# A hybrid mLSTM and gated-delta block on one core: weights loaded by half chunks, with four raw tiles and four pairs of split tiles

## The chip, the core and the metric

The kernel runs on one core of a Trainium2 chip, with its five engines: TensorE (PE in the profile, its weight loads PEld) for matrix products, VectorE (DVE), ScalarE (ACT), GpSimd (POOL) and SyncE (SP), which in this kernel issues nearly all loads of weights. Sixteen DMA engines move data between HBM and the on-chip memory SBUF. The metric is the device time of one execution in microseconds; lower is better.

## The reference, cut to what matters

One layer with 256 tokens and a width of 2048, in 32-bit floats:

```
mod = silu(c) @ W_ada + b_ada          # 6 x 2048 numbers: shift, scale, gate of both halves
h   = RMSNorm(x) * (1 + scale_m) + shift_m
proj = h @ w_in                        # q, k, v, output gate | conv input, z | gates | merge gates
y_a = bidirectional mLSTM(...)  @ w_branch_a     # 4 heads
y_b = bidirectional gated delta rule(...) @ w_branch_b   # 16 heads, chunks of 64 tokens
x  = x + gate_m * ((g_a * y_a + g_b * y_b) @ w_out)
hf = RMSNorm(x) * (1 + scale_f) + shift_f
x  = x + gate_f * ((silu(hf @ w_gate) * (hf @ w_up)) @ w_down)     # inner width 5632
```

A final RMSNorm follows. Every weight is read once: some 450 MB pass through SBUF in the course of the kernel. The last four of the six parts of `mod` belong to no early step, so their 64 MB of `W_ada` are read beside the other work.

## The kernel before, in words

**Products in three passes.** Each 32-bit weight is split into a high part and a low remainder. A load brings one *chunk* of 1 MB, 128 partitions of 8 KB, into a raw tile. Two *halves* of a chunk are then split one after the other: ScalarE copies a half (128x1024) to the high tile `wh`, and VectorE subtracts `wh` from the raw tile to get the low tile `wl`. The tokens are split in the same way (`hh`, `hl`). TensorE makes three products for each block: high by high, low by high, high by low.

**Two kinds of job.** `fjob` (lines 146 to 165) makes 128 columns for all tokens, with the weights as the loaded operand: 48 matmuls of 128x256 a chunk. `tjob` (from line 167) makes 512 columns with the tokens as the loaded operand, for two groups of 128 tokens: 24 matmuls of 128x512 a chunk, so 12 a half. Both are Python generators that yield after each half, and the rest of the program draws on them where TensorE needs work: the projections z, v, mb, o, ma, a and b are drawn between the steps of the gated delta rule. In names such as `wl_b12_1_8` stand the job (b, head 12, its second of three), and the block of the half (0 or 8 in an `fjob`, 0 or 2 in a `tjob`).

**Rings.** Tiles with one tag share a ring. Tag `raw` has 3 tiles of 8 KB a partition, tags `wh` and `wl` 3 tiles of 4 KB each. A tile is free again when its last reader is done: a raw tile after the second `wl` of its chunk, a `wh` and `wl` tile after the last matmul of the half. SP issues loads in a fixed order, so a load that waits for a raw tile holds all loads behind it.

**Modulation sums.** The parts of `mod` that are not needed early are 64 row products (`ada_part`, line 118): a 1 MB load into the same `raw` ring and one VectorE instruction at line 124, which multiplies 128x2048 weights by the broadcast row silu(c) and adds them up into one column of `mod`. `pump` (line 141) lets one of them follow every second or fourth chunk; at the output projection `wo` a table at line 1131 says after which halves one follows.

**Order.** What is marked with `order(...)` keeps the program's order on its engine; a planner with estimated costs sets the places of the rest, the splits among them. Number suffixes of names in an order listing rise in the order of the program's text.

**Stages.** 0 to 138 us: the first projection with the first two parts of `mod` (win0, `ra`, products at line 507). To 300: gates and the projections z0, v, mb. To 1000: the 16 heads of the gated delta rule in four groups; each group has an inverse of 64x64 matrices, which is solved on VectorE by repeated multiply and reduce (`uu`, lines 631 and 637) and finished by blocks on TensorE (lines 685 to 743). To 1225: mLSTM, and the projections yb and ya. To 1331: the output projection `wo`. To 1361: norm and transposes. To 2020: gate, up and down of the feed-forward part. Then a tail.

Of the kernel before, what the change touches and what calls it, by code (L numbers as in the profile page):

```python
# [24 lines left out]
KD = 11  # L25
GRP = 4
N0 = 4 + 3 * GRP


PK_ADAB = 0  # L30
# [22 lines left out]
def hybrid_block(ctx: ExitStack, tc: tile.TileContext, xr, nfr, crow, pk_d, cst_d, ada2, ada4, win0, winb, wint, wba, wbb, wo, wgu, wd, out, dbg=None):  # L53
    nc = tc.nc
# [22 lines left out]
    def both(x, kk):  # L77

        return x[:, kk // 2, :, kk % 2]
# [5 lines left out]
    def order(ins, yes=True):  # L85

        return tc.keep_in_program_order(ins) if yes else ins
# [23 lines left out]
    V.memset(row_c[:, D:], 1.0)  # L111
    def c_row(g):
        pc_ = acc_ps.tile([P, 512], F32, tag="acc", name=f"crow{g}")
        order(PE.matmul(pc_, ones[0:1], c1[:, g * 512 : (g + 1) * 512], start=True, stop=True))
        order(S.activation(row_c[:, g * 512 : (g + 1) * 512], pc_, AF.Silu))


    def ada_part(part, row_c):

        c0 = part * KB  # L120
        for b in range(KB):
            raw = st.tile([P, D], F32, tag="raw", bufs=3, name=f"ada{part}_{b}")
            nc.sync.dma_start(raw, ada4[part - 2, b])
            V.scalar_tensor_tensor(raw, raw, 1.0, row_c[:, :D], ALU.mult, ALU.mult, accum_out=mod[:, c0 + b : c0 + b + 1])  # L124
# [16 lines left out]
    def pump():  # L141
        count[0] += 1
        if every[0] and count[0] % every[0] == 0:
            sums()

    def fjob(name, src, done):

        ps = acc_ps.tile([P, 512], F32, tag="acc", name=f"acc_{name}")
        o = ps[:, :T]
        raw = st.tile([P, KB, P], F32, tag="raw", bufs=3, name=f"raw_{name}")  # L150
        nc.sync.dma_start(raw, src)
        for k0 in range(0, KB, 8):
            wh = st.tile([P, 8, P], F32R, tag="wh", bufs=3, name=f"wh_{name}_{k0}")
            wl = st.tile([P, 8, P], F32R, tag="wl", bufs=3, name=f"wl_{name}_{k0}")
            S.activation(wh, raw[:, k0 : k0 + 8], AF.Copy)  # L155
            V.tensor_tensor(wl, raw[:, k0 : k0 + 8], wh.bitcast(F32), ALU.subtract)  # L156
            for k in range(8):
                kk = k0 + k
                PE.matmul(o, wh[:, k], both(hh, kk).rearrange("p a b -> p b a"), start=kk == 0, stop=False)  # L159
                PE.matmul(o, wh[:, k], both(hl, kk).rearrange("p a b -> p b a"), start=False, stop=False)  # L160
                PE.matmul(o, wl[:, k], both(hh, kk).rearrange("p a b -> p b a"), start=False, stop=kk == KB - 1)  # L161
            if k0:
                pump()
                done(o.rearrange("p (b a) -> p a b", a=2))
            yield True

    def tjob(name, chunks, xh, xl, done, early=0, by_token=None, steps=1):

        raws = {}

        def halves(u, k0):
            if u not in raws:
                raws[u] = st.tile([P, 4, 512], F32, tag="raw", bufs=3, name=f"raw_{name}_{u}")
                nc.sync.dma_start(raws[u], chunks[u])
            wh = st.tile([P, 2, 512], F32R, tag="wh", bufs=3, name=f"wh_{name}_{u}_{k0}")
            wl = st.tile([P, 2, 512], F32R, tag="wl", bufs=3, name=f"wl_{name}_{u}_{k0}")
            order(S.activation(wh, raws[u][:, k0 : k0 + 2], AF.Copy), early)  # L180
            order(V.tensor_tensor(wl, raws[u][:, k0 : k0 + 2], wh.bitcast(F32), ALU.subtract), early)  # L181
# [12 lines left out]
        for n, (u, k0) in enumerate(todo):  # L194
            wh, wl = made.pop(0) if made else halves(u, k0)
            for k in range(2):
                kk = 4 * u + k0 + k
                for t in range(2):
                    order(PE.matmul(ps[t], tok(xh, kk, t), turns(wh[:, k]), start=kk == 0, stop=False), early and steps > 1)  # L199
                    PE.matmul(ps[t], tok(xl, kk, t), turns(wh[:, k]), start=False, stop=False)  # L200
                    PE.matmul(ps[t], tok(xh, kk, t), turns(wl[:, k]), start=False, stop=kk == last)  # L201
            if k0:
                pump()
                if u == len(chunks) - 1:
                    done(ps)
# [232 lines left out]
    with ExitStack() as s0:  # L438
# [17 lines left out]

        def loads(b):
            ra = [w0.tile([P, D + 2], F32, tag="ra", bufs=5, name=f"ra{b}_{i}") for i in range(2)]
            raw = st.tile([P, N0, P], F32, tag="raw", bufs=3, name=f"raw0_{b}")
            for i in range(2):  # L460
                order(nc.sync.dma_start(ra[i], ada2[b, :, i]))
            order(nc.sync.dma_start(raw, win0[b]))
            return ra, raw

        def scale(b, ra):
# [27 lines left out]
        for b in range(KB):  # L493
            if b:
                ra, raw = loads(b)
                m2 = scale(b, ra)
            order(V.scalar_tensor_tensor(x[:, b], x[:, b], m2[:, 0:1], rows, ALU.mult, ALU.mult))
            if b:
                shift(ra, m2)
            order(S.activation(x[:, b], x[:, b], AF.Identity, bias=m2[:, 1:2]))  # L500
            two = lambda a: a.rearrange("p (a b) -> p a b", a=2)
            order(S.activation(both(hh, b), two(x[:, b]), AF.Copy))
            for bb in ((b - 1,) if b < KB - 1 else (b - 1, b)):
                if bb >= 0:
                    order(V.tensor_tensor(both(hl, bb), two(x[:, bb]), both(hh, bb).bitcast(F32), ALU.subtract))
            for o in range(N0):
                PE.matmul(  # L507
                    first[o], raw[:, o], x[:, b], start=b == 0 and o % 2 == 0, stop=b == KB - 1 and o % 2 == 1
                )


# [848 lines left out]
```

## Time and profile before

| what | value |
|---|---|
| median of three runs | 2059.3 us (2053.61 to 2061.77) |
| profiled execution | 2056.24 us, its span 2054.3 us |
| busy | TensorE 1968.2 us, VectorE 1394.8, ScalarE 1054.0 |
| TensorE clock granted, mean | 0.986 |
| moved by DMA | 485.64 MB, mean 236 GB/s |

Times of the prediction's rows are microseconds from the start of the span, unless marked ns. The busy time of an engine tells little by itself here, since the stages have different limits: TensorE has no idle time to speak of from 1361 to 2020, while the DMA engines are busy for 97% of the time up to 138. A row of the view of waits reads "engine, tile, line <- what it waited for: us in all, times, the longest". A row of a table by stretches gives the length, the busy time of each engine with its number of instructions, the granted TensorE clock as a share of full speed, the busy share of the DMA engines, and GB/s.

### The profile page before, as it was taken

How to read it: one execution, taken by the hardware profiler on the slowest of the kernel's cores; microseconds unless marked ns; L12 is line 12 of the kernel's file. 1: busy time of each engine (PE TensorE's matmuls, PEld its weight loads, DVE VectorE, ACT ScalarE, POOL GpSimd, SP SyncE). 2: the span in 40 equal slices, each digit the busy share in tenths (PEclk: the TensorE clock that was granted, in tenths of full speed). 3: DMA queues.
4: the chain of work that ended last, by engine and by line, in shares of the span. 5: the costliest groups of instructions: out<-in, count | busy, mean ns of one | idle time of the engine just before them, and what ended most of it. 6: DMA issues, size and time to landing. Idle time of an engine off the chain costs nothing.

```text
span 2054.3 us, 27035 instructions
## 1 busy us (share of the span) xinstructions
PE 1968.2 (96%) x10374; PEld 1707.0 (83%) x10374; DVE 1394.8 (68%) x2059; ACT 1054.0 (51%) x1584; POOL 106.1 (5%) x205
## 2 busy tenths in 40 slices
PE   8999989999998899999999999889999999999998
PEld 6777779988987898899878787678888888888886
DVE  5787777786888588765667778766656665555554
ACT  3147547856774677466443443364444444444443
POOL 0002210010101010100200000000000000000000
PEclk9999999999999999999999999999999999999999
DMA  9986664566765565666987578756766766555654
GB/s 400 420 321 211 173 216 146 173 190 221 240 224 178 194 207 211 232 247 241 361 295 263 211 264 315 271 184 240 255 243 245 254 238 221 192 204 204 205 203 143
DMA packets 78962, 485.64 MB, mean 236 GB/s; under 512 B 10585, under 2 KB 15969, under 8 KB 24433
## 3 DMA queue, kind: packets, MB, share of 16 engines
q1 hardware_dynamic: 63360, 450.95, 60.9%
q0 software_dynamic: 8160, 17.88, 4.0%
q10 hardware_dynamic: 7314, 15.10, 1.9%
q8 instruction: 81, 1.33, 0.3%
q14 instruction: 47, 0.39, 0.0%
HBM read 467.07 MB, written 16.82 MB: 236 GB/s over the span
## 4 chain that ended last, share of the span: by engine, by line
PE 67%; DVE 13%; DMA 11%; ACT 5%; issue 3%; POOL 1%; ACTq 0%; SPq 0%; DVEq 0%; POOLq 0%
PE acc_up L201 4%; PE acc_up L199 4%; PE acc_up L200 4%; PE acc_d L200 4%; PE acc_d L201 4%; PE acc_d L199 4%; PE acc_gt L200 3%; PE acc_gt L201 3%; PE acc_gt L199 3%; DMA ra<-ada 3%; PE acc_b L161 2%; PE acc_b L159 2%; PE acc_b L160 2%; DMA ada<-ada 2%; PE acc_yb L201 1%
## 5 line engine op out<-in xcount | busy, mean ns | idle before, releaser
L181 DVE TENSOR_TENSOR wl_d<-raw_d,wh_d 128x1024 fp32r<-128x1024 f32 x88 | 107.8, 1225 | 109.1 <-ACT wh_d L180 109.1
L181 DVE TENSOR_TENSOR wl_up<-raw_up,wh_up 128x1024 fp32r<-128x1024 f32 x88 | 107.7, 1225 | 100.4 <-ACT wh_up L180 100.4
L159 PE MATMUL acc_b<-hh,wh_b 128*128 128x256 f32 x576 | 164.1, 285 | 5.8 <-ACT wh_b L155 5.8
L181 DVE TENSOR_TENSOR wl_gt<-raw_gt,wh_gt 128x1024 fp32r<-128x1024 f32 x88 | 107.8, 1225 | 83.2 <-ACT wh_gt L180 83.2
L161 PE MATMUL acc_b<-hh,wl_b 128*128 128x256 f32 x576 | 161.7, 281 | 2.0 <-DVE wl_b L156 2.0
L124 DVE SCALAR_TENSOR_TENSOR ada<-ada,crow 128x2048 f32<-128x2048 f32 x64 | 146.4, 2287 | 25.0 <-DMA ada<-ada 24.8
L160 PE MATMUL acc_b<-hl,wh_b 128*128 128x256 f32 x576 | 160.4, 279 | 0.0
L180 ACT ACTIVATE wh_d<-raw_d 128x1024 fp32r<-128x1024 f32 x88 | 92.9, 1056 | 127.9 <-PE acc_d L200 119.2
L180 ACT ACTIVATE wh_gt<-raw_gt 128x1024 fp32r<-128x1024 f32 x88 | 92.9, 1056 | 118.6 <-PE acc_gt L200 71.0
L180 ACT ACTIVATE wh_up<-raw_up 128x1024 fp32r<-128x1024 f32 x88 | 92.9, 1055 | 108.9 <-PE acc_up L200 78.2
L199 PE MATMUL acc_gt<-wh_gt,hfh 128*128 128x512 f32 x352 | 135.4, 385 | 0.0
L200 PE MATMUL acc_gt<-wh_gt,hfl 128*128 128x512 f32 x352 | 134.7, 383 | 0.1
L201 PE MATMUL acc_gt<-wl_gt,hfh 128*128 128x512 f32 x352 | 133.7, 380 | 0.0
L199 PE MATMUL acc_up<-wh_up,hfh 128*128 128x512 f32 x352 | 133.5, 379 | 0.0
L201 PE MATMUL acc_up<-wl_up,hfh 128*128 128x512 f32 x352 | 133.5, 379 | 0.0
L200 PE MATMUL acc_up<-wh_up,hfl 128*128 128x512 f32 x352 | 133.5, 379 | 0.0
L200 PE MATMUL acc_d<-wh_d,ffl 128*128 128x512 f32 x344 | 131.0, 381 | 0.0
L199 PE MATMUL acc_d<-wh_d,ffh 128*128 128x512 f32 x344 | 131.0, 381 | 0.0
L201 PE MATMUL acc_d<-wl_d,ffh 128*128 128x512 f32 x344 | 130.5, 379 | 0.0
L507 PE MATMUL first<-x,raw 128*128 128x256 f32 x512 | 114.5, 382 | 7.4 <-ACT x L500 6.8
L159 PEld LDWEIGHTS acc_b<-hh,wh_b 128*128 128x128 f32 x576 | 112.5, 195 | 6.4 <-ACT wh_b L155 6.3
L507 PEld LDWEIGHTS first<-x,raw 128*128 128x128 f32 x512 | 96.1, 190 | 25.8 <-ACT x L500 12.4
(369 smaller groups left out, 5275.9 us busy)
## 6 DMA issues: line engine op xcount, KB each, us to landing
ada<-ada SPq DMA_DIRECT2D x64, 1024.0 KB, 5.0
raw_gt<-wgu SPq DMA_DIRECT2D x44, 1024.0 KB, 5.0
raw_up<-wgu SPq DMA_DIRECT2D x44, 1024.0 KB, 4.9
raw_d<-wd SPq DMA_DIRECT2D x44, 1024.0 KB, 4.9
raw_b<-winb SPq DMA_DIRECT2D x36, 1024.0 KB, 5.4
ra<-ada SPq DMA_DIRECT2D x32, 1025.0 KB, 15.7
raw<-win SPq DMA_DIRECT2D x16, 1024.0 KB, 14.5
raw_z<-wint SPq DMA_DIRECT2D x16, 1024.0 KB, 5.8
```

Of the source, the lines that this page charges most:

```text
L124: V.scalar_tensor_tensor(raw, raw, 1.0, row_c[:, :D], ALU.mult, ALU.mult, accum_out=mod[:, c0 + b : c0 + b + 1])
L159: PE.matmul(o, wh[:, k], both(hh, kk).rearrange("p a b -> p b a"), start=kk == 0, stop=False)
L160: PE.matmul(o, wh[:, k], both(hl, kk).rearrange("p a b -> p b a"), start=False, stop=False)
L161: PE.matmul(o, wl[:, k], both(hh, kk).rearrange("p a b -> p b a"), start=False, stop=kk == KB - 1)
L180: order(S.activation(wh, raws[u][:, k0 : k0 + 2], AF.Copy), early)
L181: order(V.tensor_tensor(wl, raws[u][:, k0 : k0 + 2], wh.bitcast(F32), ALU.subtract), early)
L199: order(PE.matmul(ps[t], tok(xh, kk, t), turns(wh[:, k]), start=kk == 0, stop=False), early and steps > 1)
L200: PE.matmul(ps[t], tok(xl, kk, t), turns(wh[:, k]), start=False, stop=False)
L201: PE.matmul(ps[t], tok(xh, kk, t), turns(wl[:, k]), start=False, stop=kk == last)
L507: PE.matmul(first[o], raw[:, o], x[:, b], start=b == 0 and o % 2 == 0, stop=b == KB - 1 and o % 2 == 1)
```

## The change

A load brings half a chunk, 512 KB, and each half has a raw tile of its own: 4 tiles of 4 KB a partition in place of 3 of 8 KB. The 8 KB a partition that this frees, together, go to a fourth `wh` and a fourth `wl`. The sums of `ada_part` go by halves too: two loads, two VectorE instructions of 128x1024 into two columns of a small tile `mh`, and two additions a part. `pump` is called for each half and not for each chunk, so the sums follow at the same rate in bytes. The row of c comes in two loads, and the first projection's weight tile in two halves, of which one lies in the `raw` ring and one in the `wl` ring. The table at `wo` says now after which halves half a sum follows. The products are the same, in number and order.

In instructions: SP issues 829 loads and stores in place of 440, ScalarE's queue 51 in place of 50; VectorE has 64 more multiply-and-add instructions (631 for 567), ScalarE 72 function-table loads for 70.

At three places the order of instructions is shown. The first is ScalarE in the third group of the gated delta rule, around the split of `b13_0_0`, the first half that the job b of head 13 needs (`z2`, `UL` and `X` belong to the inverse by blocks, `cv` and `pad` to the convolution of head 12). Before:

```order
L735 ACTIVATE z2_0_6362<-pa_2_0_6364,sm8_4497 128x128
L736 ACTIVATE z2_0_6362<-pa_2_0_6364,sm8_4497 128x128
L735 ACTIVATE z2_0_6362<-pa_2_0_6364,sm9_4738 128x128
L736 ACTIVATE z2_0_6362<-pa_2_0_6364,sm9_4738 128x128
L297 ACTIVATE kq12_6187<-cv12_1_6274 128x256
L548 ACTIVATE sqkq12_6450<-kq12_6187 128x512
L292 ACTIVATE pad2_138<-acc_b12_2_6292 128x256
L155 ACTIVATE wh_b13_0_0_6376<-raw_b13_0_6374 128x1024
L294 ACTIVATE cv12_2_6355<-pad2_138,pk_74 128x256
L155 ACTIVATE wh_b13_0_8_6404<-raw_b13_0_6374 128x1024
```

After:

```order
L706 ACTIVATE X_1159<-Et2_0_6369 32x2x2x32
L707 ACTIVATE X_1159<-Et2_0_6369 32x2x2x32
L671 ACTIVATE X_1159<-cg2_6139 32x8x32 x4
L295 ACTIVATE pad0_136<-acc_b12_0_6330 128x256
L721 ACTIVATE UL_1160<-p2_2_0_6364 32x2x2x32
L297 ACTIVATE cv12_0_6415<-pad0_136,pk_74 128x256
L721 ACTIVATE UL_1160<-p2_2_0_6364 32x2x2x32 x3
L676 ACTIVATE UL_1160<-cg2_6139 32x8x32 x4
L162 ACTIVATE wh_b12_2_8_6556<-raw_b12_2_8_6554 128x1024
L162 ACTIVATE wh_b13_0_0_6606<-raw_b13_0_0_6604 128x1024
```

The split of `b13_0_0` stood behind the four `z2` steps and behind `pad2`, the copy of the last result of the job before it; it stands now ahead of them, behind the `X` and `UL` steps of that group's first pair of heads.

The second place is VectorE in the inverse of the second group, around the half `ma0_2_2` of the merge gates. Before:

```order
L637 TENSOR_TENSOR uu1_2588<-uu1_2588,utmp1_3575 64x21x10
L181 TENSOR_TENSOR wl_ma0_2_0_3775<-raw_ma0_2_3772,wh_ma0_2_0_3774 128x1024
L631 TENSOR_TENSOR utmp1_3575<-uu1_2588 64x220
L637 TENSOR_TENSOR uu1_2588<-uu1_2588,utmp1_3575 64x20x11
L631 TENSOR_TENSOR utmp1_3575<-uu1_2588 64x228
L637 TENSOR_TENSOR uu1_2588<-uu1_2588,utmp1_3575 64x19x12
L631 TENSOR_TENSOR utmp1_3575<-uu1_2588 64x234
L637 TENSOR_TENSOR uu1_2588<-uu1_2588,utmp1_3575 64x18x13
L631 TENSOR_TENSOR utmp1_3575<-uu1_2588 64x238
L637 TENSOR_TENSOR uu1_2588<-uu1_2588,utmp1_3575 64x17x14
L631 TENSOR_TENSOR utmp1_3575<-uu1_2588 64x240
L181 TENSOR_TENSOR wl_ma0_2_2_3797<-raw_ma0_2_3772,wh_ma0_2_2_3796 128x1024
```

After:

```order
L185 TENSOR_TENSOR wl_ma0_2_0_3903<-raw_ma0_2_0_3900,wh_ma0_2_0_3902 128x1024
L637 TENSOR_TENSOR utmp1_3693<-uu1_2684 64x198
L643 TENSOR_TENSOR uu1_2684<-uu1_2684,utmp1_3693 64x22x9
L637 TENSOR_TENSOR utmp1_3693<-uu1_2684 64x210
L643 TENSOR_TENSOR uu1_2684<-uu1_2684,utmp1_3693 64x21x10
L185 TENSOR_TENSOR wl_ma0_2_2_3927<-raw_ma0_2_2_3924,wh_ma0_2_2_3926 128x1024
```

The low part of `ma0_2_2` stood behind nine steps of the inverse counted from the half before it, and stands now behind four.

The third place is SP's queue at `wo`, in the second of its four jobs. Before:

```order
L177 DMA raw_o1_0_10995<-wo 128x2048
L123 DMA ada4_6_11029<-ada4 128x2048
L177 DMA raw_o1_1_11032<-wo 128x2048
L123 DMA ada4_7_11050<-ada4 128x2048
L177 DMA raw_o1_2_11069<-wo 128x2048
L123 DMA ada4_8_11087<-ada4 128x2048
```

After:

```order
L181 DMA raw_o1_0_0_11481<-wo 128x1024
L129 DMA ada4_6_1_11499<-ada4 128x1024
L181 DMA raw_o1_0_2_11502<-wo 128x1024
L129 DMA ada4_7_0_11520<-ada4 128x1024
L181 DMA raw_o1_1_0_11523<-wo 128x1024
L129 DMA ada4_7_1_11541<-ada4 128x1024
L181 DMA raw_o1_1_2_11544<-wo 128x1024
L129 DMA ada4_8_0_11562<-ada4 128x1024
```

Weights and sums take turns in both, by whole chunks before and by halves after.

The diff, cut to its core:

```diff
+NR = 4
+NW = 4
...
-    c1 = st.tile([1, D], F32, tag="raw", bufs=3, name="c1")
-    S.dma_start(c1, crow.unsqueeze(0))
+    c1 = [st.tile([1, D // 2], F32, tag="raw", bufs=NR, name=f"c1_{i}") for i in range(2)]
+    for i in range(2):
+        S.dma_start(c1[i], crow.unsqueeze(0)[:, i * D // 2 : (i + 1) * D // 2])
...
     def ada_part(part, row_c):
 
         c0 = part * KB
+        mh = cp.tile([P, 2, KB], F32, tag="mh", bufs=1, name=f"mh{part}")
         for b in range(KB):
-            raw = st.tile([P, D], F32, tag="raw", bufs=3, name=f"ada{part}_{b}")
-            nc.sync.dma_start(raw, ada4[part - 2, b])
-            V.scalar_tensor_tensor(raw, raw, 1.0, row_c[:, :D], ALU.mult, ALU.mult, accum_out=mod[:, c0 + b : c0 + b + 1])
-            yield True
-        V.tensor_tensor(mod[:, c0 : c0 + KB], mod[:, c0 : c0 + KB], pk[:, PK_ADAB + c0 : PK_ADAB + c0 + KB], ALU.add)
+            for i in range(2):
+                c = slice(i * D // 2, (i + 1) * D // 2)
+                raw = st.tile([P, D // 2], F32, tag="raw", bufs=NR, name=f"ada{part}_{b}_{i}")
+                nc.sync.dma_start(raw, ada4[part - 2, b][:, c])
+                V.scalar_tensor_tensor(raw, raw, 1.0, row_c[:, c], ALU.mult, ALU.mult, accum_out=mh[:, i, b : b + 1])
+                yield True
+        V.tensor_tensor(mh[:, 0], mh[:, 0], pk[:, PK_ADAB + c0 : PK_ADAB + c0 + KB], ALU.add)
+        V.tensor_tensor(mod[:, c0 : c0 + KB], mh[:, 0], mh[:, 1], ALU.add)
         yield True
...
-        raw = st.tile([P, KB, P], F32, tag="raw", bufs=3, name=f"raw_{name}")
-        nc.sync.dma_start(raw, src)
         for k0 in range(0, KB, 8):
-            wh = st.tile([P, 8, P], F32R, tag="wh", bufs=3, name=f"wh_{name}_{k0}")
-            wl = st.tile([P, 8, P], F32R, tag="wl", bufs=3, name=f"wl_{name}_{k0}")
-            S.activation(wh, raw[:, k0 : k0 + 8], AF.Copy)
-            V.tensor_tensor(wl, raw[:, k0 : k0 + 8], wh.bitcast(F32), ALU.subtract)
+            raw = st.tile([P, 8, P], F32, tag="raw", bufs=NR, name=f"raw_{name}_{k0}")
+            nc.sync.dma_start(raw, src[:, k0 : k0 + 8])
+            wh = st.tile([P, 8, P], F32R, tag="wh", bufs=NW, name=f"wh_{name}_{k0}")
+            wl = st.tile([P, 8, P], F32R, tag="wl", bufs=NW, name=f"wl_{name}_{k0}")
+            S.activation(wh, raw, AF.Copy)
+            V.tensor_tensor(wl, raw, wh.bitcast(F32), ALU.subtract)
...
+            pump()
             if k0:
-                pump()
                 done(o.rearrange("p (b a) -> p a b", a=2))
...
         def halves(u, k0):
-            if u not in raws:
-                raws[u] = st.tile([P, 4, 512], F32, tag="raw", bufs=3, name=f"raw_{name}_{u}")
-                nc.sync.dma_start(raws[u], chunks[u])
-            wh = st.tile([P, 2, 512], F32R, tag="wh", bufs=3, name=f"wh_{name}_{u}_{k0}")
-            wl = st.tile([P, 2, 512], F32R, tag="wl", bufs=3, name=f"wl_{name}_{u}_{k0}")
+            raw = st.tile([P, 2, 512], F32, tag="raw", bufs=NR, name=f"raw_{name}_{u}_{k0}")
+            nc.sync.dma_start(raw, chunks[u][:, k0 : k0 + 2])
+            wh = st.tile([P, 2, 512], F32R, tag="wh", bufs=NW, name=f"wh_{name}_{u}_{k0}")
+            wl = st.tile([P, 2, 512], F32R, tag="wl", bufs=NW, name=f"wl_{name}_{u}_{k0}")
...
             ra = [w0.tile([P, D + 2], F32, tag="ra", bufs=5, name=f"ra{b}_{i}") for i in range(2)]
-            raw = st.tile([P, N0, P], F32, tag="raw", bufs=3, name=f"raw0_{b}")
+            raw = [
+                st.tile([P, N0 // 2, P], F32, tag=("raw", "wl")[i], bufs=(NR, NW)[i], name=f"raw0_{b}_{i}") for i in range(2)
+            ]
...
-            if i in ((4, 6, 7), (1, 2, 4, 6), (1, 2, 4, 6), (1, 2, 4))[g]:
+            if i in ((2, 3, 4, 5, 6, 7), range(8), range(8), range(5))[g]:
                 sums()
```

More of the change, by code (lines that the diff above doesn't have):

```diff
@@ L113, in c_row @@
         pc_ = acc_ps.tile([P, 512], F32, tag="acc", name=f"crow{g}")
-        order(PE.matmul(pc_, ones[0:1], c1[:, g * 512 : (g + 1) * 512], start=True, stop=True))
+        order(PE.matmul(pc_, ones[0:1], c1[g // 2][:, g % 2 * 512 : (g % 2 + 1) * 512], start=True, stop=True))
         order(S.activation(row_c[:, g * 512 : (g + 1) * 512], pc_, AF.Silu))
@@ L167, in tjob @@
     def tjob(name, chunks, xh, xl, done, early=0, by_token=None, steps=1):
[L172 removed]
         def halves(u, k0):
[L175 to L181 removed]
+            raw = st.tile([P, 2, 512], F32, tag="raw", bufs=NR, name=f"raw_{name}_{u}_{k0}")
+            nc.sync.dma_start(raw, chunks[u][:, k0 : k0 + 2])
+            wh = st.tile([P, 2, 512], F32R, tag="wh", bufs=NW, name=f"wh_{name}_{u}_{k0}")
+            wl = st.tile([P, 2, 512], F32R, tag="wl", bufs=NW, name=f"wl_{name}_{u}_{k0}")
+            order(S.activation(wh, raw, AF.Copy), early)
+            order(V.tensor_tensor(wl, raw, wh.bitcast(F32), ALU.subtract), early)
             return wh, wl
@@ L201, in tjob @@
                     PE.matmul(ps[t], tok(xh, kk, t), turns(wl[:, k]), start=False, stop=kk == last)
[L202 to L205, printed above, removed]
+            pump()
+            if k0 and u == len(chunks) - 1:
+                done(ps)
             yield True
@@ L458, in loads @@
             ra = [w0.tile([P, D + 2], F32, tag="ra", bufs=5, name=f"ra{b}_{i}") for i in range(2)]
-            raw = st.tile([P, N0, P], F32, tag="raw", bufs=3, name=f"raw0_{b}")
+            raw = [
+                st.tile([P, N0 // 2, P], F32, tag=("raw", "wl")[i], bufs=(NR, NW)[i], name=f"raw0_{b}_{i}") for i in range(2)
+            ]
             for i in range(2):
                 order(nc.sync.dma_start(ra[i], ada2[b, :, i]))
-            order(nc.sync.dma_start(raw, win0[b]))
+            for i in range(2):
+                order(nc.sync.dma_start(raw[i], win0[b][:, i * N0 // 2 : (i + 1) * N0 // 2]))
             return ra, raw
@@ L507, in hybrid_block @@
                 PE.matmul(
-                    first[o], raw[:, o], x[:, b], start=b == 0 and o % 2 == 0, stop=b == KB - 1 and o % 2 == 1
+                    first[o], raw[o // (N0 // 2)][:, o % (N0 // 2)], x[:, b], start=b == 0 and o % 2 == 0, stop=b == KB - 1 and o % 2 == 1
                 )
```

## The prediction, as it was made

> **What bounds the kernel now.** I read first the table by stages, to see where TensorE has idle time at all; the columns are the length, the busy time of PE, PEld, DVE, ACT and POOL, the granted clock, the DMA share and GB/s.
>
> ```profile
> span 2054.3 us, 27035 instructions
> ...
> 0.00:138.00 138.00, 127.88 (x555) 104.58 (x555) 93.95 (x112) 31.60 (x60) 2.41 (x12) 1.00 0.97 399
> 138.00:300.00 162.00, 151.40 (x668) 124.72 (x667) 129.04 (x267) 98.94 (x153) 29.87 (x55) 0.97 0.65 203
> 300.00:1000.00 700.00, 667.96 (x4468) 608.39 (x4466) 516.86 (x969) 456.51 (x821) 68.57 (x129) 0.99 0.64 214
> 1000.00:1225.00 225.00, 219.33 (x990) 181.18 (x991) 158.24 (x200) 98.34 (x128) 5.28 (x9) 0.98 0.74 264
> 1225.00:1331.00 106.00, 95.15 (x404) 75.94 (x402) 83.37 (x100) 40.30 (x55) 0.00 (x0) 0.97 0.83 307
> 1361.00:2020.00 659.00, 658.94 (x3077) 572.40 (x3076) 379.72 (x363) 293.33 (x312) 0.00 (x0) 1.00 0.64 225
> ```
>
> The feed-forward part (1361 to 2020) has nothing to win: TensorE is busy throughout. The first 138 us hang on the DMA engines (0.97). Between 138 and 1331 TensorE is the bound with holes. The view of TensorE's waits tells which holes are waits for a split half (`wh` or `wl`); they are these:
>
> ```profile
> PE acc_o L201 <- DVE wl_o L181: 8.3, 5, 3.3
> PE acc_b L159 <- ACT wh_b L155: 5.8, 3, 2.8
> PE acc_v L201 <- DVE wl_v L181: 5.1, 5, 2.4
> PE acc_z L201 <- DVE wl_z L181: 4.4, 6, 1.2
> PE acc_o L199 <- ACT wh_o L180: 4.0, 5, 1.9
> PE acc_ma L201 <- DVE wl_ma L181: 3.7, 2, 2.0
> PE acc_a L161 <- DVE wl_a L156: 2.7, 3, 1.5
> PE acc_z L199 <- ACT wh_z L180: 2.6, 3, 1.9
> PE acc_b L161 <- DVE wl_b L156: 2.0, 4, 0.8
> PE acc_mb L201 <- DVE wl_mb L181: 0.3, 1, 0.3
> ```
>
> They sum to 38.9 us. The same view of 1225 to 1331, the stage `wo`, holds 7.9 of them, and says what starves the splits there:
>
> ```profile
> ACT wh_o L180 <- DMA raw_o<-wo: 31.5, 8, 6.1
> ...
> PE acc_o L199 <- ACT wh_o L180: 4.0, 5, 1.9
> PE acc_o L201 <- DVE wl_o L181: 3.9, 3, 2.3
> ```
>
> So `wo` waits for loads, and the other 31.0 us for a split that is late on its engine. Such a hole costs more than its length. After the hole of 1.99 us at 457.67 the clock falls to half for 3.3 us, and so it does behind other holes; the table of these stretches:
>
> ```profile
> 457.67 0.48 PE L201 MATMUL acc_ma<-wl_ma,hh 128*128 128x512 f32 x1 [1.99 <-DVE wl_ma L181]
> ```
>
> ```profile
> 161.50:164.80 3.30, 3.30 (x9) 2.58 (x9) 3.27 (x6) 2.92 (x3) 1.48 (x2) 0.50 0.21 36
> 219.50:226.30 6.80, 6.56 (x19) 5.57 (x20) 3.69 (x12) 3.04 (x8) 0.40 (x1) 0.50 0.73 145
> 308.30:311.60 3.30, 3.30 (x10) 2.58 (x9) 2.89 (x4) 2.00 (x2) 0.00 (x0) 0.50 0.00 0
> 458.50:461.80 3.30, 3.30 (x9) 2.59 (x8) 3.20 (x7) 0.60 (x1) 0.08 (x1) 0.50 0.94 308
> 700.80:704.10 3.30, 3.30 (x17) 3.30 (x17) 0.82 (x2) 3.15 (x8) 0.00 (x0) 0.50 0.46 154
> 714.50:721.20 6.70, 6.23 (x27) 5.93 (x28) 5.16 (x7) 2.90 (x4) 0.00 (x0) 0.50 0.50 171
> 1305.00:1311.70 6.70, 6.12 (x14) 4.88 (x15) 5.67 (x6) 2.50 (x5) 0.00 (x0) 0.50 0.77 282
> ```
>
> The six ahead of `wo` last 26.7 us, the one in it 6.7. Half clock doubles the time of what TensorE does in them, so 13.4 and 3.4 us are lost.
>
> **The change, term by term.** The sum is made on the profiled execution, 2056.24 us, of which 2054.3 are the span; it lies 3.1 us under the median of the runs, so 3.1 is added at the end.
>
> *1. Deeper pairs, 138 to 1225: 44.4 us in play (31.0 + 13.4).* A fourth pair lets the splits run one half further ahead. How much that is, the products of the down projection show:
>
> ```profile
> L199 PE MATMUL acc_d<-wh_d,ffh x344: 378/379/780, 1811.3 to 2038.2; 128*128 128x512 f32 x172
> ```
>
> 344 of these are 86 halves at four each, in 226.9 us: 2.6 us of TensorE work a half. A `wl` that is late by less than 2.6 us is covered if its split moves up by a whole half. Only two rows of the list have a longest hole above that (3.3 and 2.8, the last column). The order shows the two kinds of place: `wl_ma0_2_2` (the hole of 1.99 us) passes five of the inverse's steps, `wh_b13_0_0` passes the four `z2` steps and the copy of the job before it.
>
> One hole stays: the 3.3 us of `acc_o` at 308. There VectorE sits at a transpose that waits 7.3 us for a transfer, and `wl_o` is queued behind it as before:
>
> ```profile
> DVE cg L652 <- DMA cg<-inv_d: 7.3, 1, 7.3
> ```
>
> With its clock that is 3.3 + 1.65 = 5.0, so 39.4 can be had at most, 0 at least. Job b alone has 5.8 + 2.0 of it, and the clock of the stretches at 700 and 714 (5.0), which lie beside it; there the order moves the splits by most, and I take 10 of 12.8. The rest, `v`, `z`, `o`, `ma`, `a` and `mb`, is 19.9 of holes and 6.7 of clock. Their splits stand behind chains on VectorE that the change doesn't shorten, and ahead of 300 VectorE is busy for 129 of 162 us, so that a deeper ring shifts bursts but makes no room; the move of `wl_ma0_2_2` shows some gain. I take 11 of 26.6, somewhat under half. Sum −21.
>
> The Trainium skill, "TensorE: Matmul & The Clock Gate", section "Why this matters for your kernels", asks for no idle gap over some 3 us, and Part 1 has the clock fall after an idle window of some 3.4 us. By that the only gap that counts is the one at 308, which stays, and the clock's share of term 1 (about 6 of the 21) would be nothing. The row at 457.67 speaks against it, since 1.99 us were enough there.
>
> *2. Smaller loads in the stage `wo`.* Now the ring. Weights and sums take turns in SP's queue there, half by half, so of the four raw tiles two hold weights. The load of a half must wait for the `wl` two halves before it. That loop is a landing, a `wh`, a `wl`, for two halves, against 5.2 us of products. The rows:
>
> ```profile
> L181 DVE TENSOR_TENSOR wl_d<-raw_d,wh_d 128x1024 fp32r<-128x1024 f32 x88 | 107.8, 1225 | 109.1 <-ACT wh_d L180 109.1
> L124 DVE SCALAR_TENSOR_TENSOR ada<-ada,crow 128x2048 f32<-128x2048 f32 x64 | 146.4, 2287 | 25.0 <-DMA ada<-ada 24.8
> L180 ACT ACTIVATE wh_d<-raw_d 128x1024 fp32r<-128x1024 f32 x88 | 92.9, 1056 | 127.9 <-PE acc_d L200 119.2
> ```
>
> ```profile
> raw_d<-wd SPq DMA_DIRECT2D x44, 1024.0 KB, 4.9
> raw_o<-wo SPq DMA_DIRECT2D x16, 1024.0 KB, 5.7
> gtb<-mb_d SPq DMA_DIRECT2D x4, 512.0 KB, 7.4
> gta<-ma_d SPq DMA_DIRECT2D x4, 512.0 KB, 5.3
> outT<-x SPq DMA_DIRECT2D x8, 256.0 KB, 2.4
> ```
>
> On the line from 256 KB (2.4) to 1024 KB (4.9) a load of 512 KB lands after 3.2; `wo` is slower than the down stage by 5.7 / 4.9, which makes 3.7. The two other 512 KB loads of SP take 5.3 and 7.4, from buffers in HBM and among other loads; I take 3.7, since a half should land ahead of the whole that needs 5.7 in the same place, and keep 5.3 as the upper bound. The loop is 3.7 + 1.06 + 1.22 = 6.0 us, and 7.2 where the sum of the half between them (half of 2287 and a fixed part, about 1.2) is ahead of `wl` on VectorE. Each loop is then 0.8 to 2.0 us over the 5.2. With 25 half sums among 32 weight halves there are about 12 such loops: 10 to 24 us, less one and a half halves of work (4 us) that the deeper pairs have saved up at the start: 6 to 20 us lost. Before, it was 7.9 idle and 3.4 clock, 11.3. The term lies between −5 and +9. With a landing of 5.3 the loop is 7.6 to 8.8, 29 to 43 us are over, and the term is +14 to +28. I take +3, a little over the middle of the first, since SP issues in order behind a waiting sum.
>
> The Trainium skill, "DMA: Bandwidth & Descriptors", section "Bandwidth", says to batch transfers to 1 MiB or more for three quarters of the peak rate. That speaks against every load here; and at its 341 GB/s for 1 MB against some 260 for half of that (an estimate, from 2 us and the bytes at 436 GB/s, which the skill fits on "SBUF — State Buffer", section "The DMA setup-cost knee") every load here is worse. The trace doesn't decide it, since several loads are in flight at a time. What the rule would cost is the slower case below.
>
> *3. The other stages with sums.* In 1000 to 1225 two weight halves go with one of a sum. Four tiles hold 2.7 weight halves, so the same loop of 6.0 to 7.2 us stands against 2.7 × 2.6 = 7.0: it just fits, 0, to +7 in the slower case. In the feed-forward part, at four weight halves to one, 3.2 halves stand for 8.3 us of products: hidden by them, 0. If that cover went, each 0.1 us in 264 halves would cost 26.
>
> *4. First projection.* The same bytes at 0.97 DMA share, with a load more for the row of c ahead of the first product, and rows of 4 KB for a third of the bytes. A stretch of 138 us that is 1% slower costs 1.4, so +1, 0 to +4.
>
> *5. More instructions.* 64 more multiply-and-adds, of a fixed part of about 0.15 us (wl needs 1225 ns for half the elements, twice 1225 against 2287), are 10 us on VectorE, which is busy for 1395 of 2054. They are hidden behind products except where term 1 already counts VectorE as late: +1. SP's 389 more issues wait for nothing else there: 0.
>
> Sum: −21 + 3 + 0 + 1 + 1 = −16, so 2040 for the execution and **2043 us** for the median.
>
> **Rivals.**
>
> *No gain to speak of (chance 0.27).* TensorE that gets its weights earlier comes earlier to the chains of the gated delta rule, and waits there. They have waits already:
>
> ```profile
> PE px L768 <- ACT obt L770: 4.4, 2, 4.0
> ...
> PE p L719 <- DVE pt L708: 2.2, 3, 1.0
> ```
>
> For it speaks that the holes of `b` and `ma` lie right beside these chains, and that VectorE works at 80% ahead of 300. Against it, that the two rows hold 6.6 us and the splits 31.0. Of term 1 then 4 to 7 are left, terms 2, 4 and 5 give back 5: 2057 to 2060, I say 2057.
>
> *Slower (chance 0.18).* The ring of half tiles doesn't reach from a load's issue to its split. Where sums alternate with weights, TensorE goes at the pace of the loop. Its price: `wo` +13 (a landing near 5); 1000 to 1225 +7, where 36 chunks of `yb`, `ya` and `ma` need 5.2 us each and would get 7.2 / 2.7 × 2 = 5.4; the groups of the gated delta rule from the second on, where sums follow in the same measure, lose what they would win, so that only −5 of term 1 is left; and +2 from terms 4 and 5. That is +17, 2076 us. It decides once the way from issue to the end of `wl` is well over 5.2 us in `wo`, and over 7.0 elsewhere. For it speaks that before, too, `wo` waited for DMA (31.5 us of ScalarE's waits) with 1.5 times as many bytes of raw tiles; against it, that a half tile is free after one split and not two, and that 512 KB should land sooner. By the Trainium skill's rule of 1 MiB this is the outcome to expect.
>
> **How the numbers follow.** Faster over 0.5% means under 2049, slower over 2069.6; half a percent is about what a measurement of this kernel can tell from no change. The forecast has 0.55, no gain 0.27, slower 0.18. The forecast's own range is 2024 (term 1 at −32 and `wo` at −5) to 2050. So the chances are: faster 0.53, same 0.29 (the other two cases reach a little into it), slower 0.18. The range for 8 in 10 reaches from 2024 to 2069, where the slower case begins; some 0.04 are left out below it and 0.16 above.
>
> **What would show it.** Right: in the waits of TensorE, the rows of `acc_b`, `acc_v`, `acc_z`, `acc_ma` and `acc_a` fall from 26 us to about 12, with `acc_o` at 308 still there; fewer stretches at 0.50 between 138 and 1000; loads of 512 KB that land in 3 to 4 us; in `wo` some 14 us lost, as waits of `wh_o` for `raw_o`. Wrong: the rows of `p`, `px` and `pa` grow as those of the splits fall (no gain); new waits of `acc_yb`, `acc_ya`, `acc_gt` or `acc_up` for a split, with ScalarE waiting for DMA ahead of them (slower). A first stage longer than 142 us would make term 4 wrong.

## The result, and the profile after

The changed kernel takes 2157.7 us (median; 2153.59 to 2164.65) against 2060.1 for the kernel before in the same comparison: a ratio of 1.0498, with a 95% interval from 1.0476 to 1.052. It is 98 us slower. The prediction was 2043 us, with a range from 2024 to 2069.

The page of the changed kernel begins with these totals. TensorE's busy time grew by 26 us and its idle time by some 74:

```profile
span 2154.6 us, 28020 instructions
...
PE 1994.6 (93%) x10374; PEld 1726.8 (80%) x10374; DVE 1400.5 (65%) x2191; ACT 1057.0 (49%) x1586; POOL 106.7 (5%) x205
```

The table by stages of the changed kernel, with bounds laid at the same events as before (first projection, gates and z/v/mb, gated delta rule, mLSTM with yb and ya, `wo`, norm, feed-forward part, tail), shows where they went:

```profile
0.00:139.00 139.00, 128.72 (x555) 104.79 (x555) 94.03 (x111) 31.77 (x60) 2.41 (x12) 1.00 0.98 396
139.00:300.50 161.50, 148.45 (x658) 124.05 (x657) 129.41 (x267) 101.19 (x155) 28.26 (x51) 0.96 0.65 195
300.50:1025.50 725.00, 675.70 (x4478) 616.92 (x4476) 515.76 (x1013) 455.78 (x821) 70.18 (x132) 0.97 0.66 207
1025.50:1278.50 253.00, 226.47 (x991) 184.70 (x992) 164.50 (x233) 99.02 (x129) 5.82 (x10) 0.95 0.73 240
1278.50:1396.50 118.00, 98.69 (x403) 76.30 (x401) 82.07 (x122) 40.52 (x54) 0.00 (x0) 0.96 0.81 271
1396.50:1426.50 30.00, 23.57 (x101) 18.89 (x102) 18.98 (x32) 21.50 (x41) 0.00 (x0) 0.89 0.37 105
1426.50:2120.50 694.00, 668.71 (x3086) 580.27 (x3085) 382.25 (x397) 294.68 (x313) 0.00 (x0) 0.99 0.68 215
2120.50:2154.60 34.10, 24.26 (x113) 20.92 (x111) 13.46 (x19) 12.53 (x18) 0.00 (x0) 0.92 0.35 120
```

Against the lengths before (138, 162, 700, 225, 106, 30, 659, 34.3) that is +1, −0.5, +25, +28, +12, 0, +35 and 0. Apart from the 1 us of the first stage, only stages in which modulation sums are made have lost time, and only while they are made: at the start of the second group of the gated delta rule (487 us), just as the first sum is loaded, the two kernels are 1.1 us apart, and from the ninth block of the feed-forward part on, where the sums are done, they run in step again, 100.6 us apart to the end.

Two views say what TensorE and VectorE wait for. In TensorE's waits of the changed kernel the largest row is new, and rows of the chains (`pb`, `pxa`, `p`) are new or have grown:

```profile
PE pxf L1221 <- DVE sg L1215: 25.3, 8, 4.9
PE pb L749 <- DVE r L750: 11.6, 6, 2.9
...
PE pxa L982 <- DVE hal L987: 8.1, 1, 8.1
...
PE p L725 <- DVE pt L714: 6.5, 4, 2.8
```

All of them wait for VectorE, which is not busier than before (1400.5 us for 1394.8). It stands still at the sums:

```profile
L130 DVE SCALAR_TENSOR_TENSOR ada<-ada,crow 128x1024 f32<-128x1024 f32 x128 | 156.6, 1224 | 205.2 <-DMA ada<-ada 205.2
```

VectorE was idle for 205.2 us ahead of sums whose load hadn't landed; before, it was 24.8. By stage (gated delta rule, mLSTM with yb and ya, `wo`, feed-forward part) these are 71, 53, 7 and 75 us, where they were 13, 8, 3 and 1. So the stage `wo`, which is 12 us longer, isn't held up by VectorE's waits at the sums; there ScalarE waits for weights (51.7 us for 31.5). One such place in the feed-forward part, from the timeline of the changed kernel (start, length, engine, instruction, and the idle time ahead of it):

```profile
1541.79 1.22 DVE L185 TENSOR_TENSOR wl_gt<-raw_gt,wh_gt 128x1024 fp32r<-128x1024 f32 x1
1543.04 0.33 SPq L129 DMA_DIRECT2D ada<-ada  x1
...
1544.43 1.23 DVE L185 TENSOR_TENSOR wl_gt<-raw_gt,wh_gt 128x1024 fp32r<-128x1024 f32 x1 [1.42 <-ACT wh_gt L184]
...
1549.88 1.23 DVE L130 SCALAR_TENSOR_TENSOR ada<-ada,crow 128x1024 f32<-128x1024 f32 x1 [4.23 <-DMA ada<-ada]
...
1552.17 1.28 DVE L1215 TENSOR_TENSOR sg<-sg,acc_up 128x512 f32<-128x512 f32 x2
1552.90 0.47 PE L1221 MATMUL pxf<-cst,sg 128*128 128x128 f32 x1 [4.92 <-DVE sg L1215]
```

The end of a `wl` frees a raw tile, and SP issues the sum's load at once (1543.04). VectorE has one more `wl` to make, then comes the sum: it is reached 2.6 us after the issue and stands for 4.2 us, and the product `sg`, which TensorE needs next, is queued behind it and one more `wl`. The same place before:

```profile
1454.08 1.22 DVE L181 TENSOR_TENSOR wl_up<-raw_up,wh_up 128x1024 fp32r<-128x1024 f32 x1 [1.31 <-ACT wh_up L180]
1455.33 0.33 SPq L123 DMA_DIRECT2D ada<-ada  x1
1456.67 1.23 DVE L181 TENSOR_TENSOR wl_up<-raw_up,wh_up 128x1024 fp32r<-128x1024 f32 x1 [1.37 <-ACT wh_up L180]
1459.26 1.23 DVE L181 TENSOR_TENSOR wl_up<-raw_up,wh_up 128x1024 fp32r<-128x1024 f32 x1 [1.36 <-ACT wh_up L180]
1460.40 2.28 DVE L124 SCALAR_TENSOR_TENSOR ada<-ada,crow 128x2048 f32<-128x2048 f32 x1
```

There two `wl` lie between the issue and the sum, 5.1 us, and the load has landed by then. And a load of half the size lands hardly earlier. The issues of the changed kernel, whose medians were 5.0, 5.0 and 4.9 us for 1024 KB:

```profile
ada<-ada SPq DMA_DIRECT2D x128, 512.0 KB, 5.0
...
raw_gt<-wgu SPq DMA_DIRECT2D x88, 512.0 KB, 4.5
...
raw_d<-wd SPq DMA_DIRECT2D x88, 512.0 KB, 4.5
```

TensorE's products are the same, and its extra busy time is the clock: 27 stretches at half clock, 120.6 us in all, against 13 with 58.6 us before. Half of the difference is 31 us, enough for the 26. The feed-forward part has four such stretches now, where it had none; this is the table's row for the 7 us behind the hole of 4.92 us, with a mean clock of 0.61:

```profile
1552.90:1560.00 7.10, 7.10 (x25) 6.03 (x26) 3.26 (x5) 2.25 (x3) 0.00 (x0) 0.61 0.62 203
```

### The profile page after: what moved, and what is told of

Its sections match the earlier page's. It is cut to its first block, busy times and chain, and to the rows that moved or that the text cites. A ratio compares the mean times of both kernels' runs of the same rounds, so it can differ in the third digit from the quotient of the medians.

```text
span 2154.6 us, 28020 instructions
## 1 busy us (share of the span) xinstructions
PE 1994.6 (93%) x10374; PEld 1726.8 (80%) x10374; DVE 1400.5 (65%) x2191; ACT 1057.0 (49%) x1586; POOL 106.7 (5%) x205
## 4 chain that ended last, share of the span: by engine, by line
PE 48%; DMA 26%; DVE 15%; issue 6%; ACT 5%; POOL 0%; DVEq 0%; ACTq 0%; POOLq 0%; SPq 0%
DMA ada<-ada 13%; DMA ra<-ada 6%; PE acc_d L205 3%; PE acc_d L204 3%; PE acc_d L203 3%; PE acc_gt L205 3%; PE acc_gt L203 3%; PE acc_gt L204 3%; PE acc_up L204 2%; PE acc_up L203 2%; PE acc_up L205 2%; DMA raw_o<-wo 2%; DVE ada L130 1%; PE acc_b L166 1%; PE acc_b L167 1%
## 5 line engine op out<-in xcount | busy, mean ns | idle before, releaser
L130 DVE SCALAR_TENSOR_TENSOR ada<-ada,crow 128x1024 f32<-128x1024 f32 x128 | 156.6, 1224 | 205.2 <-DMA ada<-ada 205.2
L513 PEld LDWEIGHTS first<-x,raw 128*128 128x128 f32 x512 | 96.1, 190 | 26.3 <-ACT x L506 13.9
L184 ACT ACTIVATE wh_o<-raw_o 128x1024 fp32r<-128x1024 f32 x64 | 67.6, 1057 | 100.1 <-DMA raw_o<-wo 51.7
```

Source lines behind the costliest of these rows:

```text
L130: V.scalar_tensor_tensor(raw, raw, 1.0, row_c[:, c], ALU.mult, ALU.mult, accum_out=mh[:, i, b : b + 1])
L184: order(S.activation(wh, raw, AF.Copy), early)
L513: PE.matmul(first[o], raw[o // (N0 // 2)][:, o % (N0 // 2)], x[:, b], start=b == 0 and o % 2 == 0, stop=b == KB - 1 and o % 2 == 1)
```

## The experiments

Eleven kernels were run. The prediction's theories didn't hold this loss, so the first set asked whether the ring is too short (R), whether small loads and half sums cost time whatever the ring (S), or whether the fourth pair pushes splits ahead of other chains (W).

**Six raw half tiles, three pairs (e1).** The same 48 KB a partition, shared out otherwise:

```diff
-NR = 4
-NW = 4
+NR = 6
+NW = 3
```

> The changed kernel with six raw half tiles and three pairs: 48 KB a partition as in both others, half loads and half sums kept. Theory R (the raw ring of 2 MB reaches too short: a 512 KB load takes 4.4 to 5.0 us from issue to landing, hardly less than 1 MB, and VectorE waits in order for the loads of the sums): the ring holds 3 MB again, so the loss is gone, 2050 to 2075 us, and VectorE's wait for the loads of the sums falls from 205 us to under 50. Rival S (small loads, more instructions and half sums cost time whatever the ring): 2130 us or more. Rival W (the fourth pair moves splits ahead of the steps of other chains, and those are late now): 2055 to 2075 too, but with the wait for the sums' loads still above 150.

Measured: 2127.1 us, a ratio of 1.0343 (1.0294 to 1.0391). R had put it under 2075, and S at 2130 or more, which this nearly meets. The ring did what R says for the weights: ScalarE's waits for the weights' loads, 187 us in the changed kernel (51.7 of them for `raw_o` at `wo`), sink to 14.0, of which 9.6 at `wo`. But VectorE's wait for the sums stays:

```profile
DVE ada L130 <- DMA ada<-ada: 202.7, 90, 7.2
```

R alone is refuted as the cause of most of the loss. The time is 31 us under the change, with a longer ring and one pair less; the next run parts the two.

**Four raw half tiles, three pairs (e2).** `NW = 3` alone.

> The changed kernel with three pairs in place of four, four raw half tiles kept (8 KB a partition unused). Theory R: the loss stays, 2150 to 2200 us, the wait for the sums' loads about 200 us or more. Rival W: most of the loss is gone, under 2100. Rival S: 2150 to 2170, no different from the change.

Measured: 2147.6 us, 1.0451 (1.0379 to 1.0523), with 201.8 us of VectorE's waits. This is 2 us under what R and S had said, and far from W's 2100. The fourth pair isn't the cause (W falls): without it the time is 10 us lower, and the intervals overlap. From e2 to e1 the ring alone changes, and it is worth 20 us.

**Both kernels without the sums (e3, e4).** The lines that load and add up are taken out of `ada_part`, and a copy of the bias stands in for the additions:

```diff
-                raw = st.tile([P, D // 2], F32, tag="raw", bufs=NR, name=f"ada{part}_{b}_{i}")
-                nc.sync.dma_start(raw, ada4[part - 2, b][:, c])
-                V.scalar_tensor_tensor(raw, raw, 1.0, row_c[:, c], ALU.mult, ALU.mult, accum_out=mh[:, i, b : b + 1])
```

> The changed kernel without the modulation sums of the last four parts: neither their loads nor their multiply-and-adds are made (those parts of mod hold the bias alone); all else is kept. Theory R: the loss needs the sums in the ring, so this runs at 2030 to 2050 us, within 15 us of the kernel before without its sums. Rival S with half loads alone as the cost: 2080 or more. Rival W: 2070 or more, 30 us above the kernel before without sums.

> The kernel before without its modulation sums, as in the run beside it. All theories: 2025 to 2050 us, since the sums' VectorE work (146 us) and DMA waits (25 us) were mostly beside products. The difference to the changed kernel without sums is what the fourth pair and the half loads do by themselves: my term 1 says the changed one is 10 to 25 us faster, theory W slower.

Measured: 2027.3 us for the changed kernel, 0.986 (0.9825 to 0.9895) of the kernel before with its sums, and 2011.9 us, 0.9787 (0.9752 to 0.9822), for the kernel before without sums. Both are under the expected ranges: in the kernel before, too, the sums cost more (44 us) than was thought. Of the 98 us between the two, 15 are left: the loss needs the sums. The changed one is the slower here too, which is against the gain of term 1. TensorE is busy for 11 us longer in it (1959.0 for 1948.1), with 13 stretches at half clock, 67.1 us, for 10 with 38.2. In it ScalarE waits for weights all over the projections, 91 us in all and most for `raw_ma`, in the kernel before 23; one row of each:

```profile
ACT wh_ma L179 <- DMA raw_ma<-wint: 26.0, 13, 4.9
```

```profile
ACT wh_ma L177 <- DMA raw_ma<-wint: 6.7, 2, 4.3
```

**The new theory (P).** The order of instructions says why the ring made no difference to VectorE's waits at the sums. This is VectorE in the feed-forward part around the sum `ada5_6_0`, changed kernel first, then e1:

```
L185 TENSOR_TENSOR wl_up3_0_0_13275<-raw_up3_0_0_13272,wh_up3_0_0_13274 128x1024
L185 TENSOR_TENSOR wl_up3_0_2_13293<-raw_up3_0_2_13290,wh_up3_0_2_13292 128x1024
L130 SCALAR_TENSOR_TENSOR ada5_6_0_13344,mh5_12374<-ada5_6_0_13344,crow_73 128x1024
L185 TENSOR_TENSOR wl_up3_1_0_13311<-raw_up3_1_0_13308,wh_up3_1_0_13310 128x1024
L185 TENSOR_TENSOR wl_up3_1_2_13329<-raw_up3_1_2_13326,wh_up3_1_2_13328 128x1024
```

```
L185 TENSOR_TENSOR wl_gt3_3_0_13231<-raw_gt3_3_0_13228,wh_gt3_3_0_13230 128x1024
L185 TENSOR_TENSOR wl_gt3_3_2_13249<-raw_gt3_3_2_13246,wh_gt3_3_2_13248 128x1024
L130 SCALAR_TENSOR_TENSOR ada5_6_0_13344,mh5_12374<-ada5_6_0_13344,crow_73 128x1024
L185 TENSOR_TENSOR wl_up3_0_0_13275<-raw_up3_0_0_13272,wh_up3_0_0_13274 128x1024
L185 TENSOR_TENSOR wl_up3_0_2_13293<-raw_up3_0_2_13290,wh_up3_0_2_13292 128x1024
```

The sum is written in the program behind `wl_up3_1_2` (its number is higher). The planner moves it up by two halves in the one and by four in the other, each time to the second place behind the `wl` that frees its tile (`wl_up3_0_0`, `wl_gt3_3_0`, by the semaphore that the load waits for): a longer ring frees the tile sooner, and the sum moves up by just as much. In the kernel before, the sum of 1 MB stood at the third place, two halves behind. Over the whole kernel, 89 of the 128 half sums have at most one `wl` between the issue of their load and themselves; before, 53 of the 64 sums had two or three. P says: the planner puts the sum where it takes its load as landed, after one half of work, 2.6 us, for 512 KB and two, 5.2 us, for 1 MB; the chip needs about 5 for either. VectorE keeps its order, so it stands, and everything queued behind is late.

**The sum held back in the changed kernel (e5).** One edit, four raw half tiles and four pairs kept:

```diff
-                V.scalar_tensor_tensor(raw, raw, 1.0, row_c[:, c], ALU.mult, ALU.mult, accum_out=mh[:, i, b : b + 1])
+                order(V.scalar_tensor_tensor(raw, raw, 1.0, row_c[:, c], ALU.mult, ALU.mult, accum_out=mh[:, i, b : b + 1]))
```

> The changed kernel with one edit: each half sum is held on VectorE behind the instruction that is written ahead of it (in the program's order, behind the low part of the half it follows), where the planner had moved it up by two halves. Four raw half tiles, four pairs. Theory P (the planner takes a 512 KB load as landed after one half of work, 2.6 us, where it needs about 5; VectorE then stands still at the sum, and the splits queued behind it are late): from the release of its tile to the sum are now three halves, 7.8 us, so VectorE's wait for the sums' loads falls from 205 us to under 50, and 50 to 80 of the 98 us come back: 2075 to 2110. Theory R (the ring of 2 MB is too short, wherever the sum stands): 2130 or more, with the waits of ScalarE for the weights' loads grown, since a sum's tile is held longer.

Measured: 2086.5 us, 1.0145 (1.0118 to 1.0172). 71 of the 98 us came back with one pinned line, and VectorE's wait is nearly gone:

```profile
DVE ada L130 <- DMA ada<-ada: 9.8, 14, 1.8
```

In TensorE's waits the rows of `pxf` and `pb` fall with it, from 25.3 and 11.6 us to 1.1 and 0.7. What is left is put down to R, as e6 and e9 bear out. The waits of ScalarE for weights grew from 187 to 251 us, where sums and weights share the ring, as held sums keep their tiles for longer:

```profile
ACT wh_o L184 <- DMA raw_o<-wo: 63.1, 23, 7.1
ACT wh_yb L184 <- DMA raw_yb<-wbb: 35.0, 16, 4.6
ACT wh_b L162 <- DMA raw_b<-winb: 30.5, 16, 5.3
```

**Six raw half tiles, three pairs, sums held (e6).** e1 and e5 together.

> Six raw half tiles and three pairs, with the sum held as in the run beside it. Theory P with R: both causes are gone, so 2045 to 2070 us, no different from the kernel before by more than 0.7%, VectorE's wait for the sums' loads under 30 us. If something else in half loads costs (theory S), 2090 or more.

Measured: 2036.9 us, 0.9904 (0.9878 to 0.993), 121 us under the change and 19 under the kernel before, better than P with R had said. No wait for the sums' loads is listed, and ScalarE's for weights are two rows of 2 us and this one:

```profile
ACT wh_o L184 <- DMA raw_o<-wo: 30.1, 16, 3.0
```

For each sum of the feed-forward part, the time from the issue of its load until VectorE came to it (its start, less its idle time, less the issue) has these medians: 5.1 us before, 2.6 in the change, 2.6 in e1, 7.7 in e5, 10.2 in e6. Where it is under the landing time, VectorE stands; the ring alone (e1) didn't lengthen it, the held place did.

**The kernel before, its sums held (e7).** The same edit at line 124 of the kernel before.

> The kernel before with its whole sums held in the program's order: 1 MB loads, three raw tiles, three pairs. Theory P: its 25 us of VectorE waits for the sums' loads go to under 10 and the time is the same or a little better, 2040 to 2062. If holding the sums has a cost of its own (a raw tile is held for two halves longer, the ring is shorter by that), 2065 to 2090, and e5 and e6 carry that cost too.

Measured: 2046.9 us, 0.9966 (0.9942 to 0.999); VectorE's waits fall to 5.4 us. A little is to be had there too, so holding doesn't cost by itself. The comparison with e6, 0.9904, is the worth of half tiles at the same bytes, 10 us.

**Six raw half tiles without sums (e8).**

> Six raw half tiles and three pairs, with no modulation sums of the last four parts (neither loads nor multiply-and-adds). Theory R: the 15 us between the two kernels without sums come from the ring of 2 MB, which lets ScalarE wait for weights: here 2005 to 2017 us, as the kernel before without sums (2012). If the half loads themselves cost, or the order of the splits: 2022 or more.

Measured: 2020.8 us, 0.9829 (0.9805 to 0.9853), between the two answers. The interval meets those of e3 and of e4, so whether the 15 us without sums are the ring alone stays open.

**The fourth pair, once the sums don't hide it (e9).** e5 with `NW = 3`.

> Four raw half tiles, three pairs, the half sums held in the program's order: the run with sums held (2086 us) less its fourth pair. Term 1 of the prediction (a fourth pair is worth about 20 us once nothing else is in its way): 2100 to 2112. If the fourth pair is worth nothing here, because splits wait for loads and not for a free pair: 2080 to 2093.

Measured: 2079.0 us, 1.0098 (1.0072 to 1.0123). Term 1's 2100 is far off, and so are its 20 us: the kernel without the fourth pair is 7 us lower, with intervals that just meet. From e9 to e6 the ring alone changes, and it is worth 42 us.

**Sums from the first group on (e10).** e6 with

```diff
-        every[0] = (0, 2, 2, 2)[g]
+        every[0] = 2
```

> Six raw half tiles, three pairs, half sums held, and the sums begin in the first group of the gated delta rule (a half sum after every second half there, where none was made), so that fewer are left for the output projection, where ScalarE still waits 30 us for weights. Theory R (what is left at the output projection is the competition of sums and weights for the ring): that stage falls from 168 us to 155 to 162 and the whole is 2024 to 2034. If the first group has no room on VectorE: 2036 to 2050.

Measured: 2030.9 us, 0.9864 (0.9845 to 0.9883). From the first product of the transposes ahead of `wo` to the first behind it, 155 us for 168 in e6, and 10.8 us of ScalarE's waits for `raw_o` in place of 30.1; the gated delta rule gives half of it back (7 us). It is the fastest of the kernels that make the sums, though its interval still touches that of e6.

**Half loads alone (e11).** The kernel before, with two loads of 512 KB into each raw tile of 8 KB:

```diff
-                nc.sync.dma_start(raws[u], chunks[u])
+                for q in (0, 2):
+                    nc.sync.dma_start(raws[u][:, q : q + 2], chunks[u][:, q : q + 2])
```

(and so in `fjob`).

> The kernel before with one edit: the load of a weight chunk into its 8 KB raw tile is issued as two loads of 512 KB; sums in whole loads, three raw tiles, three pairs. Theory P with R: half loads by themselves cost nothing, 2050 to 2062 us, with landing times of 4 to 5 us for 512 KB. Rival S: 2070 or more.

Measured: 2060.8 us, 1.0017 (1.0002 to 1.0032): half loads of weights by themselves cost nothing that counts. With e6, which has half loads and half sums, S falls. VectorE's wait for the sums, whole as before, rose from 24.8 to 48.2 us in this run, so not all the time that VectorE stands is lost. The landing of the half loads was between 4.1 and 5.8 us, by tile:

```profile
raw_gt<-wgu SPq DMA_DIRECT2D x88, 512.0 KB, 5.0
raw_up<-wgu SPq DMA_DIRECT2D x88, 512.0 KB, 5.0
raw_d<-wd SPq DMA_DIRECT2D x88, 512.0 KB, 4.1
```

## Why the prediction was wrong

The forecast and its sign were wrong. The rival on the slower side had the ring in it, but put it at +17 us, and VectorE's stand at the sums wasn't in it.

- **Term 1 (deeper pairs, −21) had its sign come true and no time from it.** The rows of `acc_b`, `acc_v`, `acc_z`, `acc_ma` and `acc_a` fell from 26.3 us to 14.1, where 12 had been said; these are all that are left in the changed kernel:

```profile
PE acc_v L205 <- DVE wl_v L185: 6.0, 3, 5.3
...
PE acc_z L203 <- ACT wh_z L184: 2.5, 2, 1.9
...
PE acc_ma L205 <- DVE wl_ma L185: 2.0, 1, 2.0
...
PE acc_z L205 <- DVE wl_z L185: 1.8, 1, 1.8
PE acc_a L168 <- DVE wl_a L163: 1.8, 1, 1.8
```

The holes of `acc_b` (7.8 us) are gone, but not by the fourth pair: with three pairs and half tiles they are gone too (e1, e2, e6; 0.2 us in e9). With the sums held the fourth pair does shorten the five tiles' rows, 17.0 us in e5 for 23.7 in e9, yet ScalarE waits for weights for 251 us in e5 and 148 in e9, and e5 isn't faster. What failed is the step from shorter waits for splits to a shorter time: even without sums the changed kernel is 15 us slower (e3, e4), and between 139 and 1025 us it has 11 stretches at half clock for 7 before.
- **Term 2 (`wo`, +3) had the mechanism and a size off.** It measured +12, inside its bounds of −5 to +28, with 51.7 us of ScalarE's waits for `raw_o`, as its loop says. Without sums the stage, from the last product of `ya` to its own last, is as long in the changed kernel as in the kernel before (87.5 us in e3 and e4), and from e9 to e6 the ring alone takes it from 121 to 100. The landing of 512 KB there was 4.7 us where I took 3.7: the interpolation between 256 KB and 1024 KB, across unlike transfers, was too low. With the sums held (e5) the stage is slower still.
- **Term 3 (other stages with sums, 0) is the step that failed most:** +28 for mLSTM with yb and ya, +35 for the feed-forward part, and +25 in the gated delta rule, which term 1 had down as a gain. I weighed the ring's round trip against TensorE's pace, and took the sum's own instruction as something that comes when its load has landed. But VectorE keeps its order, and the sum stood in it one `wl` behind the release of its tile, 2.6 us, against a load that I had myself at 3.2 to 3.7 and that took 5. The order was looked at for splits and for SP, not for the waiting instruction that the change made 128 of. "Hidden by products" wants a row of what is queued behind the wait, here `sg` and the splits. The signs of the slower case named waits for splits alone: `acc_yb` came (6.8 us in two rows), but the largest row, 25.3 us, waits for `sg`.
- **Term 4 (first projection, +1)** measured +1. **Term 5** has its 10 us: the sums' busy time rose from 146.4 to 156.6 us.
- **The clock went the other way.** Half of 62 us more at half clock, 31 us, came on top of the holes, by the mechanism that was to give 6 back.
- **The Trainium skill's rules.** "DMA: Bandwidth & Descriptors", section "Bandwidth", which asks for transfers of 1 MiB or more, had the sign, and 4.5 us for 512 KB beside 4.9 for 1 MB agrees that a smaller load saves little. The 260 GB/s that the prediction gives for half a megabyte don't follow from the fit it names, that of the Trainium skill's "SBUF — State Buffer", section "The DMA setup-cost knee": by an estimate from it, 2 us and 512 KB at 436 GB/s are 3.2 us or 164 GB/s, and 1 MB comes to 238. No term rests on it. As a cause the rule isn't borne out: with the same bytes in the ring, half loads took 1.0017 (e11) and were a part of the fastest kernels (e6, e10). "TensorE: Matmul & The Clock Gate", section "Why this matters for your kernels", counts only gaps over some 3 us; of the 27 stretches at half clock in the changed kernel, 15 have a longest hole of 1.7 to 2.9 us in the 7 us ahead of them, and two have none over 0.3, so the trace doesn't bear out the bound.

With three pairs throughout, the four cases stand side by side: 2147.6 us (e2, four raw halves, sums as placed), 2127.1 (e1, six), 2079.0 (e9, four, sums held) and 2036.9 (e6, six, held). Holding the sums gives back 69 us with the short ring and 90 with the long one; the ring gives back 20 with the sums as placed and 42 with them held. The two causes feed each other, so no single split of the 98 is right. That the planner's reason is an estimated landing time is read from the places it chose, one half behind for 512 KB and two for 1 MB; the estimate itself wasn't seen. That the place decides is shown, by e5 and e6.

## What to carry to other kernels

When a load is cut into smaller pieces, look on each engine at how far behind the release of its tile the instruction that reads it stands, and compare that time with the landing time in the trace, which here hardly fell with the size; an engine that keeps its order passes that wait on to all that is queued behind. A planner that moves such an instruction up can move it up further when the ring gets longer, as here, so pin the instruction before judging the ring. And before giving space to deeper split tiles, see whether the splits wait for space or for data, and whether a shorter wait there becomes a shorter time.

## What the runs showed of the hardware

Halving a load of 1 MB to 512 KB moved its landing from 4.9 to 4.5 us in the down projection, where nothing else was in flight but its neighbours, and the smallest values from 4.7 to 3.6. On a straight line through the two sizes (an estimate from these four numbers), 4.1 us of the 4.9 don't depend on the bytes by the medians, and 2.5 of the 4.7 by the smallest. The halves were issued every 2.6 us and so overlap in flight, the whole loads every 5.2; how much of the 4.5 us a neighbour adds isn't shown. The views of tile `raw_d`, before and after:

```profile
DMA to landing us min/median/max: 4.7/4.9/6.4
```

```profile
DMA to landing us min/median/max: 3.6/4.5/7.6
```
